# Eleven quadrant products among the last products of the first half, with twelve more weights split ahead and a re-ordered opening, in a single-core streaming encoder layer

## The chip, the core and the metric

One core of a Trainium2 chip runs the whole layer. The metric is the device time of one execution in microseconds (us); of several runs the median is given. A core has five engines that run side by side: TensorE (PE, with the weight load PEld shown apart), VectorE (DVE), ScalarE (ACT), GpSimd (POOL) and SyncE (SP), which here only issues loads.

## The reference, cut to what matters

```python
# x: 2048 prompt rows and 32 sample rows of 1024, all float32
h = rmsnorm(x, ln_g)
q, k, v, gA, B, C, u, gC, mA, mB = split(h @ w_in)      # 1024 x 5376
attn = window_attention(rope(rmsnorm(q)), rope(rmsnorm(k)), v, sink)
conv = causal_conv3(C * u)
yA = (attn * silu(gA)) @ w_attn_out                     # 512 x 1024
yB = (B * conv * silu(gC)) @ w_conv_out                 # 512 x 1024
r  = x + (sigmoid(mA) * yA + sigmoid(mB) * yB) @ w_o    # 1024 x 1024
y  = r + sigmoid(r @ w_ple_gate) * (p @ w_ple_proj)     # 1024 x 1024, 256 x 1024
```

It also returns the last keys and values and the last two rows of `C * u`.

## The kernel before, in words

**Arithmetic.** Each float32 operand is split into a high and a low part that PE multiplies at its fp32r rate, so one product is three matmul passes (high by high, high by low, low by high) accumulated in float32. A split is a copy on ACT (`CAST`, the high part) and a subtraction on DVE (`TENSOR_TENSOR`, the low part); in the projection these are lines 231 and 232, and line 160 is the one line of all instructions in the two stages that are planned by hand. The large products are done in Strassen's manner: a 2 by 2 product of blocks needs seven products, numbered 1 to 7, of sums of blocks. In the second half of the projection the products 2, 3 and 4 are themselves cut into quadrants ("quadrant products", letters A to G).

**Columns.** Rows of x are the moving operand. They are cut into a first half (512 columns of each block) and a second half (528, with the sample rows).

**Stage one, the opening (to about 60 us), planned by hand.** `manual_schedule` holds small generators, one for each piece of work. Each yields which engine comes next and what it needs; `go(gen, due, needs, rank)` puts one on the list, and the planner gives each engine the next instruction by due time and rank (a lower rank goes first), with its own costs (line 115 holds the cost of a POOL instruction, 2.03 for a `pow`). `todo_loads` is the list in which SP issues the loads. `wpp_piece(h)` loads and splits one of four pieces of `w_ple_proj` (tiles wppr, wpp_h); `p_row` loads and splits a row block of p; `x_row(j, k)` loads one of eight row blocks of x for column half j, squares it (sq) and adds it to the running sum of squares; when all eight are in, `stats(j)` starts: the column sum by PE (pr), the `pow` on POOL (rs), and the factors that turn x into h. `wait0` fills PE's time before that with the projection's products of p by `w_ple_proj` (pp), six matmuls each. `sums0` adds up the blocks of the projection's weights for the first group and stores four of the sums to a scratch buffer for the second half.

**Stage two, the projection (to about 890 us).** There are 21 column groups of `w_in`. `steps` is the order of products. For group i of the first half it reads

```python
for i in range(G):
    steps += [[(0, i, 7)], [(0, i, 5)]]
    steps += [[(0, i + 1, 6)]] if i + 1 < G else [[seconds.pop(0)] for _ in range(2)]
    steps += [[(0, i, 3)], [(0, i, 4)]]
```

and after it come the rest of `seconds` (the quadrant products of product 2) and the second half's others. `run_set` (line 767) issues the quadrant products, with tiles la, lb, lc at line 787; the ordinary products stand at lines 649, 651 and 654 with banks a and c and the operands x_h, x_l. A product's weight is a raw tile (wr), loaded by SP, and a split pair (w), of which there are five (`WB = 5`); SP loads eight raw quads ahead ("wf"). In the second half the rows of x are loaded again (xr) and split again while products run. Here the instructions are put in order by a scheduler with a simulated timeline of its own.

**Weights split ahead.** Some weights of stage three are split during stage two and written, high and low together, to a scratch buffer: `halves` has 24 of them (8 of `w_attn_out`, "wa", and 16 of `w_o`, "o"). `half_steps` issues for each, in four places of the order of `steps`: the load by SP, the copy on ACT, the subtraction on DVE, and the store by POOL; `stored` tells stage three that a weight can be read as a finished pair of 512 KB instead of as 256 KB that are split there.

**Stage three (to the end), planned by hand again.** Units of PE work are written out in an order (yB, pp, yA, then the products by `w_o` and `w_ple_gate`, numbered with `UO` and `UPG`, tiles xb_h, xb_l, bank b), and attention tiles are begun at planned times (`begin`), `PRE` = 8 us ahead of a tile's time, with one slot for z at a time (zq, pq). `next_loads` loads a weight as a pair or starts `split_w` when ACT is near enough to idle.

Of the kernel before, what the change touches and what calls it, by code (L numbers as in the profile page):

```python
# [7 lines left out]
F32 = mybir.dt.float32  # L8
# [22 lines left out]
AHEAD = 2  # L31
KP = 41
FIRST = 6
SECOND = 4
EPS = 1e-6
SCALE = 0.125
# [6 lines left out]
def tile_hybrid_stream_step(ctx: ExitStack, tc: tile.TileContext, x, xT, pT, wu, consts, rope, ckT, cv_dup,  # L43
# [60 lines left out]
    def cost(key, op, kw):  # L104
        if LATE["V"]:
            return cost_queue(key, op, kw)
        if op == "dma_start":
            return 0.9 if kw.get("accum_op") is not None else 0.57 if key == "G" else 0.42
        n = size(kw["out"])
        if key == "T":  # L110
            return max(0.109, 0.00044 * n + 0.0064)
        if key == "S":
            return 0.2 + 0.00082 * n + (0.13 if kw.get("accum_out") is not None else 0.0)
        if key == "G":
            return 2.03 if kw.get("op") == ALU.pow else 0.35 + 0.0021 * n
        if op == "tensor_reduce":
            return 0.08 + 0.0012 * size(kw["in_"])
        return 0.3 if n <= 16 else 0.13 + 0.0011 * n
# [162 lines left out]
        open_ = letters(gs, 3, "C") + letters(gs, 4, "C")  # L281
    rest += open_
    for i in range(G):
        steps += [[(0, i, 7)], [(0, i, 5)]]
        steps += [[(0, i + 1, 6)]] if i + 1 < G else [[seconds.pop(0)] for _ in range(2)]
        steps += [[(0, i, 3)], [(0, i, 4)]]
        while begun <= i + AHEAD and begun < G:
            steps += [[(0, begun, p)] for p in ((1,) if begun < FIRST + SECOND else (1, 2))]
            begun += 1
# [67 lines left out]
    def make_sums(g):  # L357
# [9 lines left out]
        for p, i in WS.items():  # L367
# [3 lines left out]
    halves = {("wa", n): dram.tile([P, 2, 4 * P], F32, tag=f"wa{n}", name=f"wa{n}") for n in range(8)}  # L371
    halves.update({("o", n, p): dram.tile([P, 2, 4 * P], F32, tag=f"o{n}_{p}", name=f"o{n}_{p}")
                   for n in range(4) for p in WS})

    def quad_sums(x, n):
        t = {}
# [12 lines left out]
    def half_steps(key, dst):  # L389
        name = "_".join(map(str, key))  # L390
        t = zp.tile([P, 4 * P], F32, tag="z", name=f"z{name}")
        with in_turn(nc.sync.engine):
            if key[0] == "wa":
                nc.sync.dma_start(out=t.rearrange("p (a b) -> p a b", a=4), in_=wu[UY + key[1], :, 0:4, :])
            else:
                nc.sync.dma_start(out=t, in_=quad_sum[UO, key[1]][:, WS[key[2]]])
        yield
        h = zp.tile([P, 4 * P], F32R, tag="z", name=f"h{name}")
        with in_turn(nc.scalar.engine):
            nc.scalar.copy(out=h, in_=t)  # L400
        yield
        with in_turn(nc.vector.engine):
            nc.vector.tensor_tensor(out=t.bitcast(F32R), in0=t, in1=h.bitcast(F32), op=sub)
        yield
        with in_turn(nc.gpsimd.engine):
            nc.gpsimd.dma_start(out=dst[:, 0], in_=h.bitcast(F32))
            nc.gpsimd.dma_start(out=dst[:, 1], in_=t)
        yield

    def stored(key):  # L410
        if key[0] == "q" and key[3] == 0 and key[1] < 2:
            return halves["wa", key[2] - UY]
        if key[0] == "B" and key[2] == UO and key[4] in WS:
            return halves["o", key[3], key[4]]
        return None

    def raw_key(key):
# [496 lines left out]
    def hilo0(h, lo, src, key, after=None):  # L914
        yield {"@": "S"}
        eS.copy(out=h, in_=src)
        yield {"@": "V"}
        eV.tensor_tensor(out=lo, in0=src, in1=h.bitcast(F32), op=sub)
        yield {}
        have0.add(key)  # L920
        if after:
            after()
# [8 lines left out]
    def wpp_piece(h):  # L931
        raw = quad(f"wppr{h}")
        eY.dma_start(out=raw, in_=wu[UPP + h // 2, :, 4 * (h % 2):4 * (h % 2) + 4, :])
        yield {"k": 2}
        wpp[h] = pair(f"wpp{h}")
        go(hilo0(wpp[h][0][:, :512], wpp[h][1][:, :512], raw.rearrange("p a b -> p (a b)"), ("wpp", h), lambda: free("wf")), None, None, -3 if h < 2 else -1)

    def constants():
        eY.dma_start(out=cst, in_=consts)
# [3 lines left out]
    def x_row(j, k):  # L943
        v = B[k // 4, j, k % 4] = xrow(f"b{j}_{k}")
        eY.dma_start(out=v[:, :q0], in_=xT[k * P:(k + 1) * P, j * q0:(j + 1) * q0])
        yield {"k": 1, "@": "S"}
        sq = row(f"sq{j}_{k}")[:, :q0]
        eS.activation(out=sq, in_=v[:, :q0], func=AF.Square, scale=1.0 / 32.0)
        yield {}
        if j not in acc0:  # L950
            acc0[j] = sq
        else:
            yield {"@": "V"}
            eV.tensor_tensor(out=acc0[j], in0=acc0[j], in1=sq, op=add)
            yield {}
            free("k")
        ready[j] = ready.get(j, 0) + 1
        if ready[j] == 8:
            go(stats(j), now[0] + 1.8, None, j * 2 - 3)


    def stats(j):
# [80 lines left out]
    def sums0():  # L1043
        a11, a21, a22, a12 = [quad(f"a0_{i}") for i in range(4)]
        u1, u2 = groups[0][2:]
        for t, (u, s) in zip((a11, a21, a22, a12), ((u1, 0), (u2, 0), (u2, 1), (u1, 1))):
            eY.dma_start(out=t, in_=wu[u, :, 4 * s:4 * s + 4, :])
        yield {"wf": 1}
        sc = quad("sc0")
        for o, x, y in ((sc, a11, a21), (a21, a21, a22), (a11, a11, a21), (a12, a12, a11)):  # L1050
            yield {"@": "V"}
            eV.tensor_tensor(out=o, in0=x, in1=y, op=add)
        yield {}
        sums[0] = {7: sc, 5: a21, 6: a11, 3: a12, 4: a22}
        for p, i in WS.items():
            eG.dma_start(out=wsum[0][:, i], in_=sums[0][p])
        for i in range(NP, NW):
            raw_of[i] = sums[0].pop(worder[i][3])
            go(split0(i), None, None, -0.5)
            yield {}  # L1060
# [9 lines left out]
    def split0(i):  # L1070
        while i > len(made):
# [14 lines left out]
    todo_loads = [({"tmp": 1}, (-2, p_row(0, 0))), ({"tmp": 1}, (-2, p_row(0, 1))), ({"wf": 1}, (-3, wpp_piece(0))),  # L1086
                  ({"wf": 1}, (-2, wpp_piece(1))), ({}, (-2, x_row(0, 0))), ({}, (-2, x_row(0, 1))), ({}, (-2, x_row(0, 2))),
                  ({}, (0, constants())), ({"wf": 1}, (-2, wpp_piece(2)))]
    todo_loads += [({}, (-2, x_row(0, k))) for k in range(3, 8)] + [({"wf": 1}, (-1, wpp_piece(3)))]
    todo_loads += [({"wf": 1}, (0, raw0(i))) for i in range(2)] + [({"tmp": 1}, (0, p_row(1, k))) for k in range(2)]  # L1090
    todo_loads += [({"wf": 1}, (0, raw0(i))) for i in range(2, 5)]
    todo_loads += [({}, (1, x_row(1, k))) for k in range(8)]
    todo_loads += [({"wf": 1}, (-1.5, raw0(i))) for i in range(5, 9)] + [({"wf": 4}, (-0.5, sums0()))]
# [144 lines left out]
    for p, at_ in ((2, (0, G - 1, 2)), (1, (1, pairs_[1], 2, "E")), (6, (1, pairs_[3], 2, "E")), (7, (1, pairs_[5], 2, "E")),  # L1238
# [12 lines left out]
                (spans[0][0] + pitch * j for j in range(len(halves)))]  # L1251
    half_at = sorted((t + lag, j, k) for j, t in enumerate(split_at) for k, lag in enumerate((-11, -2.5, 0.1, 1.0)))
    half_gen = [half_steps(*x) for x in halves.items()]
    conv_at = {(1, G - 2, 1): lambda: conv_load(0), (1, G - 2, 6): lambda: (conv_split(0), conv_load(1)),
               (1, G - 1, 6): lambda: conv_split(1), (1, G - 2, 5): lambda: conv_load(2)}
    conv_at.update({(1, sets[-1], 3 + c % 2, "DE"[c // 2]): lambda c=c: conv_split(2, (c,)) for c in range(4)})
    prep = [at_step[0, g, 7] for g in range(7, G)]
    for i, todo in enumerate(steps):
        if i < NS:
            continue  # L1260
        if todo[0][:2] == (0, 0) and todo[0][2] in (3, 4):
            make_x(todo[0][2])
        run(todo)
        if todo[0] in conv_at:
            conv_at[todo[0]]()
        if i in prep:
            next(X1, None)
        if todo[0] in sums_at:
            quad_sums(*sums_at[todo[0]])
        while half_at and length[i] and half_at[0][0] <= sum(length[:i]):  # L1270
            next(half_gen[half_at.pop(0)[1]])
        if i in after:
            load_second_products(after[i])
        if i in refills:
            if refills[i] == 2:
                for _ in X1:
                    pass
            refill(refills[i])
# [715 lines left out]
    def next_loads():  # L1994
# [36 lines left out]
        while n_split[0] < len(worder) and room["w"] > 0:  # L2031
            i = n_split[0]
            src = stored(worder[i])
            if src is not None:
                if busy["Y"] >= now[0] + 0.5:
                    break
                room["w"] -= 1
                w = wp.tile([P, 2, 4, P], F32R, tag="w", name=f"w{i}")
                W2[i] = w[:, 0], w[:, 1]
                fin[0] = 0.0  # L2040
                eY.dma_start(out=w.bitcast(F32).rearrange("p a b c -> p a (b c)"), in_=src)
                w_ready[i] = fin[0] + 0.5
            else:
                if landed.get(i, 1e9) > now[0] or busy["S"] >= now[0] + (0.3 if i > used[0] + 2 else 1.5):
                    break
                room["w"] -= 1
                go(split_w(i))
            n_split[0] += 1
# [55 lines left out]
    left.update({0: 4, 1: 4, 2: 5, 3: 5})  # L2104
    for e in range(len(TILES)):
        t = (0, 6)[e] if e < 2 else 11 * e if e < 8 else e1 - 40 + 0.96 * (e2 - e1) * (e - 8) / 9
        begin.append((max(0.0, t - PRE), lambda e=e, t=t: go(attention(e, t), None, {"z": 1, "tmp": 2})))
    begin.append((T["yB0_6"], lambda: load_p(2)))
    begin.append((T["yB0_7"], lambda: load_p(3)))
    begin.append((T["yB0_0"], lambda: load_conv(3)))  # L2110
# [103 lines left out]
```

## Time and profile before

| | |
|---|---|
| device time, median of 3 runs | 1509.16 us (1509.11 to 1510.27) |
| profiled execution, its own time | 1508.07 us |
| its span, from first to last instruction | 1506.0 us |
| mean granted TensorE clock | 0.998 of full speed |
| busy: PE, weight load | 1489.3, 1348.6 us |
| busy: DVE, ACT, POOL | 1210.7, 803.7, 399.0 us |
| moved by DMA | 378.34 MB, mean 251 GB/s |

How to read it: a row of the timeline has the start, the length, the engine, the line, the operation, what it writes and reads, its shape and how many in a row, and in brackets the idle time before it with what ended it. A row of the groups has the number of instructions, busy time and mean duration in ns, and the idle time before them with what ended most of it. A row of the windows has a stretch, its length, the busy time of PE, weight load, DVE, ACT and POOL with the number of instructions of each, the granted clock, the DMA share and GB/s. The releaser of a wait is inferred from semaphore events.

### The profile page before, as it was taken

What the parts mean: (1) busy time and instruction counts of PE and PEld (TensorE: products, weight loads), DVE (VectorE), ACT (ScalarE), POOL (GpSimd) and SP (SyncE); (2) the same over time, 40 slices, a digit from 0 to 9 for tenths busy, and PEclk for the clock granted to TensorE, in tenths of its full rate; (3) what the DMA queues carried; (4) which work ended last, traced back from release to release, by engine and by line L of the source; (5) the groups of instructions that cost most, each with busy time, mean ns of one, the idle gap of its engine ahead of it and who ended that gap; (6) DMA issues with size and microseconds to landing.
All of it is one profiled execution on the core that took longest, in us unless ns stands there. A gap on an engine that the chain in (4) does not pass through costs nothing.

```text
span 1506.0 us, 28005 instructions
## 1 busy us (share of the span) xinstructions
PE 1489.3 (99%) x9553; PEld 1348.6 (90%) x9553; DVE 1210.7 (80%) x2308; ACT 803.7 (53%) x1910; POOL 399.0 (26%) x582
## 2 busy tenths in 40 slices
PE   9999999999999999999999999999999999999998
PEld 7878888888889999999999989998888788999998
DVE  7897887885579788799976878778899999676777
ACT  8453244344457655434455646687765686342453
POOL 2133332332211443433323311113232202211201
PEclk9999999999999999999999999999999999999999
DMA  9469886898777987533578885687988959989959
GB/s 353 154 246 348 314 291 221 276 347 271 253 274 256 340 292 262 186 127 122 153 243 312 288 270 181 210 253 218 302 207 272 240 157 258 312 247 283 256 168 286
DMA packets 206670, 378.34 MB, mean 251 GB/s; under 512 B 24896, under 2 KB 58496, under 8 KB 206528
## 3 DMA queue, kind: packets, MB, share of 16 engines
q1 hardware_dynamic: 160608, 258.30, 52.6%
q0 software_dynamic: 36272, 100.44, 22.2%
q10 hardware_dynamic: 9648, 17.83, 3.2%
q8 instruction: 75, 1.23, 0.3%
q14 instruction: 67, 0.55, 0.1%
HBM read 246.53 MB, written 130.04 MB: 250 GB/s over the span
## 4 chain that ended last, share of the span: by engine, by line
PE 91%; DMA 4%; DVE 2%; ACT 1%; issue 1%; POOL 0%; SPq 0%; DVEq 0%; ACTq 0%; POOLq 0%
PE b L160 21%; PE a L654 8%; PE a L651 7%; PE a L649 7%; PE yB L160 6%; PE yA L160 5%; PE la L787 5%; PE c L651 4%; PE c L649 4%; PE c L654 4%; PE lc L787 2%; PE pp L160 2%; PE O L160 2%; PE S L160 2%; PE PT L160 1%; PE lb L787 1%
## 5 line engine op out<-in xcount | busy, mean ns | idle before, releaser
L160 PE MATMUL b<-xb_h,w 128*128 128x264 f32 (+1 forms) x1344 | 310.7, 322 | 1.4 <-DVE at L160 1.4
L160 PEld LDWEIGHTS b<-xb_h,w 128*128 128x128 f32 x1344 | 222.7, 188 | 19.5 <-DVE at L160 1.9
L651 PE MATMUL a<-x_l,w 128*128 128x264 f32 (+1 forms) x744 | 228.2, 320 | 0.0
L649 PE MATMUL a<-x_h,w 128*128 128x264 f32 (+1 forms) x744 | 227.4, 320 | 0.2 <-ACT w L231 0.2
L160 PE MATMUL b<-xb_l,w 128*128 128x264 f32 (+1 forms) x672 | 216.6, 322 | 0.0
L654 PE MATMUL a<-x_h,w 128*128 128x264 f32 (+1 forms) x744 | 199.7, 321 | 0.9 <-DVE w L232 0.9
L231 ACT CAST w<-wr 128x512 fp32r<-128x512 f32 (+1 forms) x180 | 110.5, 619 | 96.2 <-PE c L654 34.9
L232 DVE TENSOR_TENSOR w<-wr,w 128x512 fp32r<-128x512 f32 (+1 forms) x180 | 133.2, 748 | 29.6 <-ACT w L231 28.0
L649 PEld LDWEIGHTS a<-x_h,w 128*128 128x128 f32 x744 | 139.9, 188 | 11.3 <-ACT w L231 0.4
L651 PEld LDWEIGHTS a<-x_l,w 128*128 128x128 f32 x744 | 140.0, 188 | 10.9
L654 PEld LDWEIGHTS a<-x_h,w 128*128 128x128 f32 x744 | 124.0, 188 | 11.9 <-DVE w L232 1.2
L160 PEld LDWEIGHTS b<-xb_l,w 128*128 128x128 f32 x672 | 126.4, 188 | 8.5
L160 ACT CAST w<-wr 128x512 fp32r<-128x512 f32 x120 | 73.6, 622 | 98.4 <-PE b L160 51.5
L787 PE MATMUL la<-x_h,w 128*128 128x264 f32 x516 | 111.3, 285 | 1.6 <-ACT w L231 1.6
L651 PE MATMUL c<-x_l,w 128*128 128x512 f32 (+1 forms) x336 | 110.9, 340 | 0.0
L649 PE MATMUL c<-x_h,w 128*128 128x512 f32 (+1 forms) x336 | 110.5, 339 | 0.0
L231 ACT CAST w<-a 128x512 fp32r<-128x512 f32 x82 | 49.8, 620 | 98.6 <-DVE a L364 33.2
L654 PE MATMUL c<-x_h,w 128*128 128x512 f32 (+1 forms) x336 | 100.1, 339 | 0.0
L160 DVE TENSOR_TENSOR w<-wr,w 128x512 fp32r<-128x512 f32 x120 | 83.6, 705 | 18.0 <-ACT w L160 17.7
L848 DVE SCALAR_TENSOR_TENSOR u<-u,c 128x264 f32<-128x264 f32 (+1 forms) x125 | 59.5, 507 | 42.8 <-ACT u L843 26.1
L160 PE MATMUL yB<-ycs_h,w 128*128 128x264 f32 (+1 forms) x384 | 91.0, 325 | 0.0
L160 PE MATMUL yA<-ac_h,w 128*128 128x264 f32 (+1 forms) x384 | 90.5, 323 | 0.0
(443 smaller groups left out, 3889.7 us busy)
## 6 DMA issues: line engine op xcount, KB each, us to landing
wr<-in_wu SPq DMA_DIRECT2D x161, 256.0 KB, 4.8
a<-in_wu SPq DMA_DIRECT2D x116, 256.0 KB, 5.3
wr<-ws SPq DMA_DIRECT2D x74, 256.0 KB, 4.0
w<-o SPq DMA_DIRECT2D x32, 512.0 KB, 4.7
ws<-a POOLq DMA_DIRECT2D x63, 256.0 KB, 4.3
w<-wa SPq DMA_DIRECT2D x16, 512.0 KB, 5.3
wr<-qs SPq DMA_DIRECT2D x32, 256.0 KB, 4.0
qs<-a POOLq DMA_DIRECT2D x24, 256.0 KB, 5.8
```

The costliest lines, as they stand in the source:

```text
L160: return f(**kw)
L231: nc.scalar.copy(out=hi, in_=src)
L232: nc.vector.tensor_tensor(out=lo, in0=src, in1=hi.bitcast(F32), op=sub)
L649: nc.tensor.matmul(out=ps[:, :cn], lhsT=w[:, 0, k], rhs=x[0][:, c0:c0 + cn], start=first and k == 0, stop=False, skip_group_check=True)
L651: nc.tensor.matmul(out=ps[:, :cn], lhsT=w[:, 0, k], rhs=x[1][:, c0:c0 + cn], start=False, stop=False, skip_group_check=True)
L654: nc.tensor.matmul(out=ps[:, :cn], lhsT=w[:, 1, k], rhs=x[0][:, c0:c0 + cn], start=False, stop=k == 3, skip_group_check=True)
L787: nc.tensor.matmul(out=ps[:, :m], lhsT=w[:, a, k], rhs=r[:, cols], start=q in "ABG" and j == 0 and e == 0, stop=j == 1 and e == 2, skip_gr ...
L848: nc.vector.scalar_tensor_tensor(out=t[:, c0:c0 + cn], in0=t[:, c0:c0 + cn], scalar=-1.0, in1=ps[:, :cn], op0=mul, op1=sub)
```

## The change

- **The order of `steps`.** In the last group of the first half, eleven quadrant products of `seconds` stand behind product 7 (three), 5 (four) and 3 (four); there were two, behind product 5.
- **Weights split ahead.** `halves0` adds twelve (four blocks each of three of the weights of `w_o` and `w_ple_gate`) that stage three uses for its first column half. Their four steps are spread between product 7 of group 14 and product 5 of the last group, with the load four steps ahead, the copy one step ahead, and the subtraction and store at the place.
- **The opening.** All four pieces of `w_ple_proj` have rank -3 (the last two had -1), and the fourth is loaded ahead of the last two row blocks of x; the p rows of block 1 come before the first raw weights. Two of the first eight squares are made on DVE. `stats` is put on the list for 0.3 us after the last sum instead of 1.8. The four stores of `sums0` become a generator of their own with rank 2. The planner's cost of a `pow` goes from 2.03 to 1.1 in this stage.
- **Stage three.** A weight that is needed next may be split when ACT is busy up to 5.0 us ahead (1.5 before), and attention tiles 0 to 2 are begun 11 us ahead of their time instead of 8.

```diff
+H0 = 14
+EARLY = (3, 4, 4, 0)
...
-            return 2.03 if kw.get("op") == ALU.pow else 0.35 + 0.0021 * n
+            return 1.1 if kw.get("op") == ALU.pow else 0.35 + 0.0021 * n
...
     for i in range(G):
-        steps += [[(0, i, 7)], [(0, i, 5)]]
-        steps += [[(0, i + 1, 6)]] if i + 1 < G else [[seconds.pop(0)] for _ in range(2)]
-        steps += [[(0, i, 3)], [(0, i, 4)]]
+        for p, n in zip((7, 5, 3, 4), EARLY if i + 1 == G else (0, 0, 0, 0)):
+            steps += [[(0, i, p)]] + ([[(0, i + 1, 6)]] if p == 5 and i + 1 < G else [[seconds.pop(0)] for _ in range(n)])
...
+    RAW = {1: 0, 4: 1}
+    halves0 = {(x, n, p): dram.tile([P, 2, 4 * P], F32, tag=f"r{x}{n}_{p}", name=f"r{x}{n}_{p}")
+               for x, p in ((UO, 1), (UO, 4), (UPG, 1)) for n in range(4)}
...
+            elif key in halves0:
+                u, e = key[0] + key[1] + 4 * (key[2] == 4), RAW[key[2]]
+                nc.sync.dma_start(out=t.rearrange("p (a b) -> p a b", a=4), in_=wu[u, :, 4 * e:4 * e + 4, :])
...
+        if key[0] == "B" and key[1] == 0:
+            return halves0.get(key[2:])
         return None
...
-        go(hilo0(..., ("wpp", h), lambda: free("wf")), None, None, -3 if h < 2 else -1)
+        go(hilo0(..., ("wpp", h), lambda: free("wf")), None, None, -3)
...
-        yield {"k": 1, "@": "S"}
+        vector = j == 0 and k in (2, 5)
+        yield {"k": 1, "@": "V" if vector else "S"}
         sq = row(f"sq{j}_{k}")[:, :q0]
-        eS.activation(out=sq, in_=v[:, :q0], func=AF.Square, scale=1.0 / 32.0)
+        if vector:
+            eV.scalar_tensor_tensor(out=sq, in0=v[:, :q0], scalar=1.0 / 1024.0, in1=v[:, :q0], op0=mul, op1=mul)
+        else:
+            eS.activation(out=sq, in_=v[:, :q0], func=AF.Square, scale=1.0 / 32.0)
...
-            go(stats(j), now[0] + 1.8, None, j * 2 - 3)
+            go(stats(j), now[0] + 0.3, None, j * 2 - 3)
...
         sums[0] = {7: sc, 5: a21, 6: a11, 3: a12, 4: a22}
-        for p, i in WS.items():
-            eG.dma_start(out=wsum[0][:, i], in_=sums[0][p])
+        kept = dict(sums[0])
+
+        def keep():
+            for p, i in WS.items():
+                eG.dma_start(out=wsum[0][:, i], in_=kept[p])
+                yield {"@": "G"}
+        go(keep(), None, None, 2)
...
-    todo_loads += [({}, (-2, x_row(0, k))) for k in range(3, 8)] + [({"wf": 1}, (-1, wpp_piece(3)))]
-    todo_loads += [({"wf": 1}, (0, raw0(i))) for i in range(2)] + [({"tmp": 1}, (0, p_row(1, k))) for k in range(2)]
+    todo_loads += [({}, (-2, x_row(0, k))) for k in range(3, 6)] + [({"wf": 1}, (-2, wpp_piece(3)))]
+    todo_loads += [({}, (-2, x_row(0, k))) for k in (6, 7)] + [({"tmp": 1}, (-1, p_row(1, k))) for k in range(2)]
+    todo_loads += [({"wf": 1}, (0, raw0(i))) for i in range(2)]
...
+    gen0 = [half_steps(*x) for x in halves0.items()]
+    first0, last0 = at_step[0, H0, 7], at_step[0, G - 1, 5]
+    pitch0 = (last0 - first0) / (len(gen0) - 1)
+    at0 = sorted((first0 + pitch0 * j + lag, j) for j in range(len(gen0)) for lag in (-4, -1, 0, 0.4))
...
+        while at0 and at0[0][0] <= i:
+            next(gen0[at0.pop(0)[1]])
...
-                if landed.get(i, 1e9) > now[0] or busy["S"] >= now[0] + (0.3 if i > used[0] + 2 else 1.5):
+                if landed.get(i, 1e9) > now[0] or busy["S"] >= now[0] + (0.3 if i > used[0] + 2 else 1.5 if i > used[0] + 1 else 5.0):
...
-        begin.append((max(0.0, t - PRE), lambda e=e, t=t: go(attention(e, t), None, {"z": 1, "tmp": 2})))
+        begin.append((max(0.0, t - (PRE if e > 2 else 11.0)), lambda e=e, t=t: go(attention(e, t), None, {"z": 1, "tmp": 2})))
```

More of the change, by code (lines that the diff above doesn't have):

```diff
@@ L935, in wpp_piece @@
         wpp[h] = pair(f"wpp{h}")
-        go(hilo0(wpp[h][0][:, :512], wpp[h][1][:, :512], raw.rearrange("p a b -> p (a b)"), ("wpp", h), lambda: free("wf")), None, None, -3 if h < 2 else -1)
+        go(hilo0(wpp[h][0][:, :512], wpp[h][1][:, :512], raw.rearrange("p a b -> p (a b)"), ("wpp", h), lambda: free("wf")), None, None, -3)
     def constants():
```

## The prediction

> **What bounds the kernel now.** The page first: the busy line, then the chain, then the list of what the matmul engine (PE) waited for.
>
> ```profile
> PE 1489.3 (99%) x9553; PEld 1348.6 (90%) x9553; DVE 1210.7 (80%) x2308; ACT 803.7 (53%) x1910; POOL 399.0 (26%) x582
> PE 91%; DMA 4%; DVE 2%; ACT 1%; issue 1%; POOL 0%; SPq 0%; DVEq 0%; ACTq 0%; POOLq 0%
> PE la L787 <- ACT w L231: 1.6, 2, 1.1
> PE b L160 <- DVE at L160: 1.4, 1, 1.4
> PE pp L160 <- ACT wpp_h L160: 1.4, 1, 1.4
> PE pq L160 <- DMA zq<-z_q: 1.2, 1, 1.2
> PE 1_0_461 L649 <- ACT x_h L160: 1.0, 1, 1.0
> PE lc L787 <- ACT w L231: 1.0, 3, 0.4
> ```
>
> The reader is to see that PE is busy for 1489.3 of 1506.0 us and owns 91% of the chain. The edit takes no matmul away, so all it can win is waiting: the six rows add up to 7.6 us, half a per cent. A change of 0.2% (3.0 us) is about what a measurement of this kernel can tell from none. Each part is therefore held against one of these rows.
>
> **The change part by part.** 1. The opening: the fourth piece of w_ple_proj is loaded two places earlier, all pieces get rank -3, two of the first eight squares go to DVE, and the sum of squares (pr) is planned 1.5 us sooner. The row aimed at is the wait for wpp_h.
>
> ```profile
> 14.40:16.86 2.46, 1.08 (x5) 0.60 (x5) 1.97 (x4) 2.46 (x6) 1.43 (x3) 1.00 1.05 398
> 18.00:21.40 3.40, 3.40 (x10) 2.63 (x9) 2.84 (x6) 1.86 (x4) 2.01 (x3) 0.50 1.05 410
> 4.49 4.04 SPq L160 DMA_DIRECT2D b<-in_xT  x5
> 8.88 0.33 SPq L160 DMA_DIRECT2D wppr<-in_wu  x1
> 8.21 5.40 DMA b<-in_xT
> 10.93 0.63 ACT L160 ACTIVATE sq<-b 128x512 f32<-128x512 f32 x1
> 14.98 0.69 DVE L160 TENSOR_TENSOR sq<-sq,sq 128x512 f32<-128x512 f32 x1
> 15.12 0.62 ACT L160 CAST wpp_h<-wppr 128x512 fp32r<-128x512 f32 x1
> 15.79 0.50 PE L160 MATMUL pp<-p_h,wpp_h 128*128 128x512 f32 x1 [1.38 <-ACT wpp_h L160]
> 16.86 0.95 PE L160 MATMUL pr<-ones,sq 128*128 128x1 f32 x8
> 38.96 1.89 DVE L160 TENSOR_TENSOR w<-wr,w 128x512 fp32r<-128x512 f32 x3
> 40.77 0.68 DVE L160 TENSOR_TENSOR sc<-a,a 128x512 f32<-128x512 f32 x1
> ```
>
> The windows read: length, then busy time of PE, weight load, DVE, ACT, POOL, granted clock, DMA share, GB/s. The eighth row of x was issued at 8.21 and landed at 13.61 (8.21+5.40); the fourth, squared from 10.93, had landed by then, so a load lands every 0.67 us. With wpp moved up two places it lands near 12.9 and is split by about 14.8: PE gets it without a wait. But the last row of x now lands at 14.28, and the squares on DVE stand in DVE's list ahead of sums and of that split. From the sixth row of x on (12.3), DVE has seven operations left: square, two sums, the split, three sums. Back to back, three such operations take 1.89 where one takes 0.68: (1.89-0.68)/2 = 0.61 apart. Seven end at 12.3+6x0.61+0.69 = 16.65, say 16.7. Before, the last sum ended at 14.98+0.69 = 15.67. So pr, at 16.86 now, can run at 16.7: 0.15 us better. PE would do better only if more projection products stood ahead of pr. I followed the planner's own event times by hand, for the order and not for a time: the DVE squares delay its sum by about what the lag gives back, and pr comes behind 39 projection matmuls again. The wait moves from wpp_h to the squares. Bounds: a gain of 1.4 plus the slow clock below; a loss of 0.5, two matmuls of 0.23 fewer ahead of pr. I take -0.15, nearest the DVE rows.
>
> From 18.00 to 21.40 the granted clock is 0.50, and ten 512-column matmuls take what would be half the time: about 1.6 us lost, right after the wait. With a wait of like length I leave it as it is. The Trainium skill (TensorE: Matmul & The Clock Gate, "What's actually happening") says that the clock halves after an idle window of about 3.4 us; the length of the slow stretch agrees with that, but 1.4 us of wait were enough here, so the measurement decides. By the page's rule closing the wait would return the wait alone.
>
> 2. The second column half: pow is planned at 1.1 us, stats(1) 1.5 us sooner, and the four stores of sums stand behind it on POOL (keep), no longer ahead. These stores issue later and nobody waits for them.
>
> ```profile
> 18.24 1.27 POOL L160 TENSOR_TENSOR rs<-rs,nhalf 128x4 f32<-128x4 f32 x1
> 47.47 0.16 DVE L160 TENSOR_SCALAR rs<-pr 128x4 f32<-128x4 f32 x1 [2.88 <-PE pr L160]
> 55.53 0.69 DVE L160 TENSOR_TENSOR s<-2_3_764,s 128x512 f32<-128x512 f32 x1 [3.15 <-issue]
> 55.50:83.00 27.50, 27.50 (x120) 22.17 (x119) 27.25 (x45) 13.96 (x26) 2.70 (x5) 1.00 0.33 116
> 84.62 0.50 PE L649 MATMUL 1_0_461<-x_h,w 128*128 128x512 f32 x1 [1.02 <-ACT x_h L160]
> ```
>
> pow really takes 1.27, so 1.1 is nearer than 2.03. DVE idles 2.88 and 3.15 us around this chain and is then full (27.25 of 27.50) until PE waits at 84.62. Starting the chain 2.4 us sooner (1.5+0.9) fills that idle time; the two squares cost DVE 1.4 us, but before 17 us. The wait of 1.02, with 0.16 of refill, should go: -1.2 (bounds 0 and -1.2).
>
> 3. Eleven quadrant products (there were two) among the last group's products.
>
> ```profile
> 440.00:457.90 17.90, 17.90 (x118) 16.39 (x118) 13.73 (x28) 12.19 (x27) 0.00 (x0) 1.00 0.64 214
> 457.90:473.10 15.20, 15.20 (x125) 15.17 (x124) 14.67 (x34) 10.98 (x27) 3.25 (x6) 1.00 0.75 255
> 473.10:500.00 26.90, 24.36 (x185) 22.91 (x184) 25.82 (x57) 19.98 (x49) 8.06 (x11) 1.00 0.77 258
> 465.93 0.41 ACT L231 CAST w<-wc 128x256 fp32r<-128x256 f32 x1 [1.05 <-PE la L787]
> 491.88 0.64 ACT L231 CAST x_h<-xr 128x528 fp32r<-128x528 f32 x1 [3.39 <-DMA xr<-xc]
> ```
>
> PE loses 2.54 us, from 473.1 on, where DVE is full (25.82 of 26.90) and ACT stands before refilled rows. Where the products are moved (440 to 457.9) PE loses nothing. After the twelfth quadrant product the order is what it was and PE has done the same work. Could DVE have run ahead meanwhile? No: only five weight buffers exist, and at 465.93 ACT still waits for PE to give one back. So the head start can't be stored: 0. Bounds -2.54 and, if the denser splits before 458 cost as much as afterwards (2.54 in 26.9), +1.7 in 17.9.
>
> 4. Twelve more weights split ahead, in groups 14 to 20, read as pairs in the third stage.
>
> ```profile
> 316.00:442.00 126.00, 126.00 (x543) 101.62 (x542) 82.35 (x140) 56.38 (x99) 32.38 (x60) 1.00 0.84 290
> 420.00:440.00 20.00, 20.00 (x87) 16.16 (x87) 16.18 (x33) 11.77 (x22) 4.29 (x8) 1.00 0.98 342
> L160 ACT CAST w<-wr 128x512 fp32r<-128x512 f32 x120 | 73.6, 622 | 98.4 <-PE b L160 51.5
> L160 DVE TENSOR_TENSOR w<-wr,w 128x512 fp32r<-128x512 f32 x120 | 83.6, 705 | 18.0 <-ACT w L160 17.7
> 1180.00:1220.00 40.00, 38.58 (x204) 32.32 (x203) 39.48 (x79) 29.47 (x78) 8.94 (x10) 1.00 0.69 173
> 1203.94 0.50 PE L160 MATMUL b<-xb_h,w 128*128 128x512 f32 x1 [1.43 <-DVE at L160]
> ```
>
> Added in 126 us: 12 x 0.622 = 7.5 us of ACT (56.38 busy), 12 x 0.705 = 8.5 of DVE (82.35 busy), 24 POOL issues, and 12 x 768 KB = 9.4 MB, 75 GB/s on 290. All fits; only 420 to 440 would come to 417, just over the 410 seen at 18 us. Price 0, bounds 0 and +5 (below). In the third stage the same ACT and DVE work goes, against 12 x 256 KB more to load. DVE is full there (39.48 of 40), and PE's one long wait, 1.43 plus 0.16 of refill, is for a late DVE read of a bank. Less DVE work makes it likelier on time, but the planner rewrites the order from there: half of 1.6, -0.8 (bounds 0 and -1.6).
>
> 5. Attention is begun 11 us ahead for the first three tiles: the first two begin at zero either way, and the third needs the single z slot, which the second holds until the first is through. 0; the wait for zq stays. The looser rule for splitting a weight needed next: 0, as no row of the third stage shows PE waiting for a split.
>
> Sum: -0.15-1.2+0+0-0.8 = -2.15. Against the profiled execution, 1508.07, that is 1505.9; it stands 1.09 under the median of the three runs, 1509.16, so 1507.0.
>
> **The rivals.** A. The opening closes. For it: ACT, the engine named, is relieved, and if pr falls seven matmuls later PE covers the sum. Against it: the DVE count. It returns 1.4 and, if the slow clock goes with it, 1.6: 1504.0. By the page's rule on the clock it would be 1505.6.
>
> B. The second half's waits go. For it: DVE works 13.73 of 17.90 us before them, so 4 us lie free. Against it: the five buffers. 2.54 back: 1504.5.
>
> C. Slower: the early splits arrive late. ACT takes its list in order, and an early split's copy waits for its own load as the copy at 491.88 did (3.39). The load is placed three steps ahead of the copy, and in the last group three steps are quadrant products of 0.73 us, not products of 2.8. It decides when ACT stands longer than the five buffers hold out, some 8 us; two such copies, with traffic over 410 GB/s, reach that and cost about 5 us: 1512.2. The Trainium skill (DMA: Bandwidth & Descriptors, "Issuing engines are not separate DMA queues") speaks for C: stores issued by POOL share the engines with SP's loads. No row here separates the two.
>
> D. It gains nothing: each wait removed (84.62, 1203.94) comes back one place later, and the opening loses its 0.5: 1509.6.
>
> **How the numbers follow.** My forecast 0.50, A 0.18, B 0.12, C 0.10, D 0.10. Faster by over 0.2% (under 1506.1): A and B, 0.30, and 0.05 of my own case, whose range is 1505.5 to 1508.5. Slower (over 1512.2): 0.08 of C. The range, 1503.5 to 1510.5, holds my case, D, A and B each alone, and leaves out C and A with B together.
>
> **What would show it.** Step 1: PE's row waiting for wpp_h is gone, one for the squares stands before pr near 15 to 16.7, and the clock is still 0.50 for 3.4 us; if PE is full to 18, A holds. Step 2: no wait at the first L649 product of 1_0, and DVE's 2.88 and 3.15 shorter. Step 3: PE waits from about 470 to 500 as before; under 1 us there means B. Step 4: no PE wait from 316 to 460, ACT waits on the new loads at most 3 us; the wait near 1200 shorter. Step 5: pq still waits for zq near 885. I am wrong most easily where an order is rewritten: the opening's pr, and the third stage.

## The result and the profile after

The changed kernel took 1533.2 us in the median of 4 runs (1528.8 to 1535.5), against 1509.13 us for the kernel before: 1.0157 times as long, 95% interval 1.013 to 1.0183, some 24 us slower. The forecast was 1507.0 us, with 1503.5 to 1510.5 as its range. Two executions of later kernels ran far slower than the rest (4554.15 us with four weights split ahead, 2438.25 us with eight), and the ratios leave them out.

Page of the changed kernel, span and busy line:

```profile
span 1533.7 us, 28071 instructions
PE 1499.8 (98%) x9553; PEld 1354.2 (88%) x9553; DVE 1212.4 (79%) x2310; ACT 801.4 (52%) x1908; POOL 410.1 (27%) x606
```

PE does the same 9553 matmuls, so the time must lie between them. A sum finds the places: for each matmul, the distance from its start to the next one's, less the median distance of its shape. By it the kernel before loses 18.6 us in its execution and the changed one 46.8, and most of the difference sits in few places (its profiled execution, 1535.51 us, was the slowest of the four):

| stretch (us) | lost before | lost after |
|---|---|---|
| 0 to 150 (opening and first products) | 7.8 | 8.0 |
| 400 to 450 (last group of the first half) | -0.1 | 10.4 |
| 450 to 550 (quadrant products) | 5.2 | 4.9 |
| 1100 to 1200 | 0.4 | 2.8 |
| 1200 to 1300 (third stage) | 1.6 | 14.5 |

First place. The timeline of the changed kernel, what PE, ACT and SP did in the last group:

```profile
428.67 0.90 SPq L631 DMA_DIRECT2D xq<-xc  x2
434.94 0.33 SPq L353 DMA_DIRECT2D wr<-in_wu  x1
436.69 0.33 SPq L353 DMA_DIRECT2D wb<-in_wu  x1
437.14 0.84 SPq L649 DMA_DIRECT2D xr<-xc  x2
441.97 0.63 ACT L233 CAST x_h<-xr 128x528 fp32r<-128x528 f32 x1 [6.03 <-DMA xr<-xc]
442.65 0.59 PE L796 MATMUL la<-x_h,w 128*128 128x264 f32 x1 [7.37 <-ACT x_h L233]
447.99 0.63 PE L663 MATMUL a<-x_h,w 128*128 128x512 f32 x1
```

The kernel before, the same loads and its first quadrant product:

```profile
422.32 0.96 SPq L622 DMA_DIRECT2D xq<-xc  x2
424.19 0.33 SPq L352 DMA_DIRECT2D wb<-in_wu  x1
427.39 0.33 SPq L352 DMA_DIRECT2D wr<-in_wu  x1
427.83 0.87 SPq L640 DMA_DIRECT2D xr<-xc  x2
442.13 0.28 PE L787 MATMUL la<-x_h,w 128*128 128x264 f32 x1
```

The first quadrant product (tile la) needs rows of the second half (xr), loaded by SP. Before, they were issued at 427.83, 14 us ahead of their use at 442.13. After, the product is asked for at 435, right behind product 7, and the rows are issued at 437.14: counted from the first load for the row sums (xq, at 419.13 before and 420.43 after), SP's list holds six weight loads ahead of them where it held four. The last two, at 434.94 and 436.69, wait 6.9 us together, by the profile for DVE to give back raw buffers. PE stands 7.37 us and then runs slowly to about 448.4 (a 512-column matmul is shown with 0.63, not 0.40, and the next starts after 0.43, not 0.23; the granted clock was 0.63 from 434.8 to 448.4).

Second place. Third stage of the changed kernel, 30 us before its longest wait (columns as in the prediction), then the timeline:

```profile
1180.00:1210.00 30.00, 29.41 (x147) 24.14 (x146) 18.72 (x36) 14.26 (x39) 9.26 (x10) 1.00 1.08 320
```

```profile
1203.40 0.68 DVE L162 TENSOR_TENSOR c<-c,b 128x512 f32<-128x512 f32 x1
1213.06 0.69 DVE L162 TENSOR_TENSOR c<-c,c 128x512 f32<-128x512 f32 x1 [8.98 <-DMA z_r<-c]
1215.93 0.42 DVE L162 TENSOR_TENSOR ptl<-PT,pth 128x256 fp32r<-128x256 f32 x1
1216.40 0.58 PE L162 MATMUL O<-ptl,VH 128*128 128x256 f32 x1 [6.09 <-DVE ptl L162]
1281.80 0.80 PE L162 MATMUL b<-xb_h,w 128*128 128x512 f32 x1 [2.42 <-DVE c L162]
```

The kernel before, the same 30 us of work:

```profile
1175.00:1205.00 30.00, 28.57 (x147) 23.75 (x146) 29.52 (x56) 19.57 (x53) 8.02 (x8) 1.00 0.90 225
```

DVE is relieved as foreseen (18.72 of 30 us, it was 29.52), but the traffic has gone from 225 to 320 GB/s and the DMA share from 0.90 to 1.08. DVE now stands 8.98 us at a row c until a store from it (z_r<-c), as the profile infers, has landed, and `ptl`, which PE needs, stands behind that in DVE's list. SP issues this store, so it does not issue loads alone. The chain back from PE's wait has the store behind the landing of a new pair (w<-r):

```profile
1192.16 9.00 DMA w<-r
1201.22 11.71 DMA z_r<-c
```

The second wait, 2.42 us at 1281.80 and a stretch at half clock after it, stands by the same chain behind a store to the output that took 8.59 us from 1272.35. The last new pair had landed at 1214.88, so its bytes were not under way then; what makes this store late is open. The DMA view of the 50 us around these stretches, first before, then after, has the median time from issue to landing as its last figure:

```profile
wr<-qs SPq DMA_DIRECT2D x12, 256.0 KB, 3.9
z_r<-c SPq DMA_DIRECT2D x11, 256.0 KB, 4.0
c<-in_xT POOLq DMA_DIRECT2D x9, 256.0 KB, 5.2
```

```profile
w<-r SPq DMA_DIRECT2D x8, 512.0 KB, 8.9
c<-in_xT POOLq DMA_DIRECT2D x12, 256.0 KB, 7.0
z_r<-c SPq DMA_DIRECT2D x9, 256.0 KB, 7.1
wr<-qs SPq DMA_DIRECT2D x9, 256.0 KB, 9.5
```

Eight of the twelve new pairs (w<-r) fall into this stretch, and the transfers shown beside them take longer: a store 7.1 us where it took 4.0.

### The profile page after: what moved, and what is told of

Its sections match the earlier page's. It is cut to its first block, busy times and chain, and to the rows that moved or that the text cites. A ratio compares the mean times of both kernels' runs of the same rounds, so it can differ in the third digit from the quotient of the medians.

```text
span 1533.7 us, 28071 instructions
## 1 busy us (share of the span) xinstructions
PE 1499.8 (98%) x9553; PEld 1354.2 (88%) x9553; DVE 1212.4 (79%) x2310; ACT 801.4 (52%) x1908; POOL 410.1 (27%) x606
## 5 line engine op out<-in xcount | busy, mean ns | idle before, releaser
L234 DVE TENSOR_TENSOR w<-wr,w 128x512 fp32r<-128x512 f32 (+1 forms) x180 | 136.9, 770 | 36.6 <-ACT w L233 36.4
L162 ACT CAST w<-wr 128x512 fp32r<-128x512 f32 x108 | 66.8, 623 | 98.6 <-PE b L162 53.7
L796 PEld LDWEIGHTS la<-x_h,w 128*128 128x128 f32 x516 | 87.1, 189 | 10.5 <-ACT x_h L233 7.8
```

The source lines that it names most:

```text
L162: return f(**kw)
L234: nc.vector.tensor_tensor(out=lo, in0=src, in1=hi.bitcast(F32), op=sub)
L796: nc.tensor.matmul(out=ps[:, :m], lhsT=w[:, a, k], rhs=r[:, cols], start=q in "ABG" and j == 0 and e == 0, stop=j == 1 and e == 2, skip_gr ...
```

## The experiments

The theory to be tested: the wait at 435 comes from the eleven products and the splits together, by the order of SP's list; the waits of the third stage come from reading the pairs where the DMA engines are full. Times below are medians of 4 to 11 runs; ratios are to the kernel before in the same series, where it took 1508.3 to 1509.4 us. The changed kernel's own ratio, 1.0157, is known to some 4 us either way, and so is each difference to it.

**Without the early products.**

```diff
-EARLY = (3, 4, 4, 0)
+EARLY = (0, 2, 0, 0)
```

> The changed kernel with the order of products of before (two quadrant products behind product 5 of the last group); the twelve splits and all else stay. In the changed kernel PE waits 7.4 us at 434.9 for x_h of the first quadrant product: the rows for it (xr) are issued by SP at 437.1, where before issued them at 427.8. Theory T: that wait needs both, products asked for some 15 us sooner and rows loaded 9 us later behind weight loads because the splits hold row tiles; so here the rows come at about 437 as well but the first quadrant product is due only near 450, and the wait (with its slow clock 10.4 us) is gone; the waits of the third stage (8.8 at 1210, 5.7 at 1279) stay. About 1525 us. Rival R1, the products alone are too early: the same here, 1525. Rival R2, the twelve splits by themselves starve the last group: a wait of several us stays near 435 to 450, 1530 or more.

1524.69 us, ratio 1.0102 (1.0089 to 1.0115). The stretch 400 to 450 loses 3.0 us in place of 10.4, none of it in a wait for rows: xr is issued at 429.9. Third-stage waits of 6.1 and 2.0 us are there, as in the changed kernel (6.1 and 2.4). T holds in the time and in the wait that is gone, but not in its reason: the rows do not come at 437, so the early products also push their own rows back in SP's list.

**Without the splits.**

```diff
-               for x, p in ((UO, 1), (UO, 4), (UPG, 1)) for n in range(4)}
+               for x, p in () for n in range(4)}
...
-    pitch0 = (last0 - first0) / (len(gen0) - 1)
+    pitch0 = 0.0
```

> The changed kernel without the twelve new splits (neither made nor read); eleven products stay among the last group's. Theory T: SP issues xr near 428 again, PE waits at most 1 us at 435; third stage without the waits at 1210 and 1279, since the pairs of 512 KB that crowd the DMA queues there are not read. About 1507 to 1509 us. Rival R1 (the products are asked for before their rows can be there, splits or not): a wait of 5 us or more at 435, about 1517. Rival R3 (the waits of the third stage come from the attention tiles begun 11 us ahead or from the looser split rule): they stay, about 1522.

1508.98 us, ratio 0.9996 (0.9987 to 1.0005). SP issues xr at 428.54, PE loses nothing from 400 to 450, and 1.6 us from 1200 to 1300 as before. R1 and R3 fall. The eleven products alone bring nothing that can be measured.

**Without both.** The last two edits together.

> The changed kernel without the splits and with the order of products of before: only the opening, the attention lead and the split rule are left of the change. Theory T: 1506 to 1509 us, no wait at 435, none over 2 us in the third stage. Rival R3: the third stage's 14 us stay, about 1522.

1506.76 us, ratio 0.9990 (0.9981 to 0.9999). With before's order of products or the new one, with the splits or without, four kernels make a square: the early products cost 1.0157 less 1.0102, some 8 us, beside the splits, and 1 us or nothing without them; the splits cost 17 us without the early products and 24 with them.

**Splits made, not read.** The two lines that hand the new pairs to the third stage are left out:

```diff
-        if key[0] == "B" and key[1] == 0:
-            return halves0.get(key[2:])
```

> The changed kernel makes and stores the twelve splits, but the third stage loads and splits these weights itself as before. Theory T: the waits at 1210 and 1279 (14.5 us) are gone, the wait at 435 (10.4 us with its slow clock) stays: about 1519 us. Rival R3: both stay, 1533. Rival R4, making them costs the third stage too (they shift the state in which it begins): in between, over 1523.

1517.4 us, ratio 1.0051 (1.0038 to 1.0064). The waits in the third stage are those of the kernel before (1.33 us at 1213), the one at 435 stays:

```profile
439.92 0.59 PE L794 MATMUL la<-x_h,w 128*128 128x264 f32 x1 [6.12 <-ACT x_h L233]
1215.14 0.50 PE L162 MATMUL b<-xb_h,w 128*128 128x512 f32 x1 [1.33 <-DVE at L162]
```

So reading the pairs costs 1.0157 less 1.0051, 16 us; making them beside the early products costs 8 us. R3 and R4 fall.

**Rows ahead of the last row sums.**

```diff
+            refill(refills[i])
             if refills[i] == 2:
                 for _ in X1:
                     pass
-            refill(refills[i])
```

> The changed kernel, but the rows for the first quadrant products (xr) are loaded before the last two row sums (xq, which serve a later product), no longer behind them. In SP's list xr then stands behind the weight load wr_4260 and ahead of five more weight loads; in the changed kernel it stands behind those five, two of which wait for a weight buffer that PE gives back. Theory T, the wait at 434.9 (7.4 us, 10.4 with the slow clock) is SP's order: xr goes out before 425, the wait is under 1 us, about 1523 to 1524 us, with the third stage's 14.5 us unchanged. Rival R6, the loads are slow because the splits fill the DMA engines in the last group: xr goes out early and still lands after 440, the wait stays over 4 us, 1529 or more.

1525.92 us, ratio 1.0117 (1.0103 to 1.013). SP's list and PE's one wait here:

```profile
418.70 0.93 SPq L649 DMA_DIRECT2D xr<-xc  x2
```

```profile
438.54 0.55 PE L658 MATMUL a<-x_h,w 128*128 128x512 f32 x1 [1.97 <-ACT u L852]
```

The rows go out 18 us sooner, under no less traffic (319 GB/s from 418 to 442, in the changed kernel 292), and the wait for them is gone: SP's order was its cause, R6 falls. (The two loads that hold up the rows in the changed kernel wait for DVE by the profile, not for PE as I had expected.) It was not all: a wait of 1.97 takes its place further on, for a bank that ACT empties (u) behind a weight whose sum DVE made late; the stretch loses 3.9 us, not under 1.

**Splits sooner.**

```diff
-H0 = 14
+H0 = 8
...
-    first0, last0 = at_step[0, H0, 7], at_step[0, G - 1, 5]
+    first0, last0 = at_step[0, H0, 7], at_step[0, 17, 5]
```

> The changed kernel with its twelve splits spread over groups 8 to 17 of the first half, no longer 14 to 20; all of them are read. SP's list in the last group then is that of the kernel without splits. Theory T: the wait at 434.9 falls under 1 us, the waits near 1200 (8.8) and 1270 (5.7) stay: 1523 to 1524 us. Rival R7, it is not where the splits stand but that they exist (more waits in groups 8 to 17): 1527 or more.

1523.5 us, ratio 1.01 (1.0086 to 1.0114). xr is issued at 427.99 and the stretch 400 to 450 loses 0.1 us; one new wait of 1.25 us at 320; the third stage loses 17 us from 1150 to 1300. T holds, R7 falls.

**High halves alone.** The low halves of the new pairs are not read; the high ones are used in their place.

```diff
+                if worder[i][2:] in halves0 and worder[i][1] == 0:
+                    W2[i] = w[:, 0], w[:, 0]
+                    eY.dma_start(out=w[:, 0]..., in_=src[:, 0])
+                else:
...
```

> The changed kernel, but of the twelve new pairs the third stage reads only the high halves (256 KB, as many bytes as a raw weight) and multiplies by them in place of the low ones as well; so ACT and DVE are spared as before and PE does as much, but 3 MB less is read. Theory T: the waits at 1210 and 1279 (14.5 us) come from the DMA engines, full at 320 GB/s from 1180 to 1210; both fall under 2 us each and the time is about 1519 to 1520 us. Rival R5, they come from the order that the planner makes when these splits are missing (DVE's list waits for a row c whatever the traffic): they stay, about 1533.

1520.18 us, ratio 1.0081 (1.0067 to 1.0094): by the ratios 11.5 us less than the changed kernel, with ACT and DVE still spared. Part of that lies elsewhere (in the profiles the opening and the stretch at 435 lose 2.8 us less). From 1100 to 1300 this kernel loses 8.5 us, the changed one 17.3, the one whose pairs are not read 2.7: 9 of 15 us are back. The wait at 1210 shrinks to 1.98 us, the one at 1279 is gone:

```profile
1209.32 0.39 PE L162 MATMUL O<-ptl,VH 128*128 128x256 f32 x1 [1.98 <-DVE ptl L162]
1178.00:1208.00 30.00, 28.92 (x146) 23.86 (x144) 23.61 (x45) 13.77 (x37) 10.10 (x10) 1.00 1.06 294
```

The stretch is still full (1.06, 294 GB/s), for even as 256 KB the pairs come beside raw weights for products eleven places on. The bytes are not the only thing that changed: the planner counts a load's bytes, so SP's list has another order here, and so have the other engines' lists before 1180 and after 1217 (times of the changed kernel). Between these, up to the wait at 1210, DVE and PE have the same instructions in the same order. The store at which DVE stood 8.98 us now takes 7.68 us to land, not 11.71, and is issued 5.4 us before DVE comes to it, not 2.9; DVE stands 2.43 us. So 4.0 of the 6.55 us that DVE is spared are shorter landing, the rest is SP's new order. R5, that the waits stay whatever the traffic, falls; how much of the second wait is bytes and how much order is not shown.

**Four, four others, eight of the twelve.** All with the order of products of before and the splits in groups 8 to 17; the list of weights is `(UO, 1)`, `(UPG, 1)`, or `(UO, 1), (UO, 4)`.

> The order of products of before; only the four weights of w_o's product 1 are split ahead, in groups 8 to 17, and read as pairs near 1100, where before the DMA share was 0.70 at 176 GB/s. The opening and the third stage's rules as in the changed kernel. Theory T: pairs cost nothing where the DMA engines have room, and nothing waits for the splits: no wait over 2 us at 435, 1200 or 1270, about 1506 to 1508 us (the kernel without any of the splits took 1506.8). Rival R8, any pair more costs the third stage: 1510 or more.

1509.97 us, ratio 1.0007 (0.9998 to 1.0016): no gain and no measurable loss against the kernel before. No wait at 435, and none of over 2 us near 1200 or 1270, but one of 2.24 us at 1234. The time lies between T's (to 1508) and R8's (from 1510), and settles neither.

> The order of products of before; only w_ple_gate's product 1 (four weights) split ahead and read as pairs, in the second half of the stretch from 1175 to 1210. Theory T: as with the other four, 1510 to 1515 us. Rival R11: 1519 or more.

1512.79 us, ratio 1.0027 (1.0017 to 1.0038). One wait, of the kind of the changed kernel, 3.98 us at 1198; traffic from 1180 to 1200 is 297 GB/s at a share of 0.99. T's time holds, R11 falls.

> The order of products of before; eight weights (w_o's products 1 and 4) split ahead in groups 8 to 17 and read as pairs; w_ple_gate's product 1 is loaded and split as before. Four pairs in the stretch from 1175 to 1210 where the changed kernel has eight. Theory T: half the added traffic (about 270 GB/s), so less than half of the 14 us: 1510 to 1515 us. Rival R11, the order that the planner makes is the cause, any such weight missing from DVE's list brings the wait: 1519 or more.

1513.58 us, ratio 1.003 (1.0018 to 1.0042); waits of 0.3 to 2.0 us from 1186 to 1262. R11 falls. By the ratios, four pairs near 1100 cost 2.6 us against the kernel without splits, four more near 1180 another 3.5, and the last four on top of these (the kernel without early products, which has twelve but makes them later) about 11. Of these 11, 3.0 are lost at 400 to 450, where the later splits are made; from 1100 to 1300 the losses go from 7.3 to 14.8. The price rises as the stretch fills.

**Raw weights later.**

```diff
-    LEAD, LOOK, SLACK = 2, 11, 1.5
+    LEAD, LOOK, SLACK = 2, 6, 1.5
```

with the splits in groups 8 to 17, and with the early products or the order of before:

> The changed kernel with its twelve splits in groups 8 to 17, all read as pairs, and with raw weights of the third stage loaded 6 weights ahead, no longer 11. In the changed kernel eight pairs are loaded from 1179 to 1204, among them nine raw weights for products up to eleven places later; with 6 most of these come after the pairs, where the traffic had fallen to 126 GB/s (1220 to 1240). Theory T (what hurts is that pairs and later raw weights fall together): 1180 to 1210 goes from 320 to 260 to 290 GB/s, the third stage's waits from 14 to 17 us down to under 6, about 1511 to 1514 us. Rival R9, the pairs alone are too much there, whatever is loaded beside them: 1520 or more. Rival R10, six ahead is too late for raw weights: new waits of PE for weights elsewhere in the third stage.

> The same with the order of products of before. Eleven quadrant products among the others were worth nothing where their rows came in time (0.9996 of before, against 0.9990 with the order of before), so this is within 2 us of the kernel above, whichever theory holds.

1522.47 us, ratio 1.0092 (1.0079 to 1.0105), and 1517.76 us, ratio 1.0055 (1.0043 to 1.0067). This expectation failed. The losses from 1150 to 1300 do fall, from 17 us (splits sooner) to 7, but not by less traffic, so why is open. One of the two times meets R9's 1520, the other does not. In the first, a wait for a raw weight comes in, as R10 had it (ACT stands up to 3.7 us at such a load, DVE behind ACT, PE behind DVE):

```profile
1180.00:1200.00 20.00, 15.88 (x75) 12.79 (x74) 14.11 (x28) 6.94 (x17) 4.91 (x5) 1.00 1.08 338
1330.51 0.81 PE L162 MATMUL b<-xb_h,w 128*128 128x264 f32 x2 [2.80 <-DVE w L162]
```

The two also differ by 4.7 us where I had expected at most 2: in the profiles, 2.6 us among the quadrant products and 3.5 us from 1300 to 1350. In the third stage the two have all but the same order of instructions, so what the early products have to do with the second is open.

No version clearly beats the kernel before. The best, without both, is 0.1% faster, and its interval ends at 0.9999.

## Why the prediction was wrong

**Step 4 failed: its price of 0 for making the splits, and its gain of 0.8 for reading them, were the largest errors.** It weighed the ACT and DVE work of the splits and found both had room, which was right in the main. Two things were left out:

- *Reading.* "12 x 256 KB more to load" was set down and not placed. I showed the window 1180 to 1220, with a share of 0.69, and took the stage by it; the 30 us before its longest wait stood at 0.90, and eight of the twelve loads fall there. The step named DVE as what bounds that stage. DVE was relieved of work, and then stood for stores that land late (11.71 us for the one behind the longest wait). Measured: 16 us for reading the pairs. With half the bytes, 9 of the 15 us lost in the third stage are back, in part through SP's order. The -0.8 that I had booked as a gain is part of that error.
- *Queues moved past.* The splits' loads and their tiles change the order of SP's list in the last two groups. I counted "24 POOL issues" and 75 GB/s, not who stands behind whom on SP. Measured: 8 us, beside the early products.

**Step 3: 0 is right for the products alone** (ratio 0.9996 with, 0.9990 without), and the stretch 450 to 550 loses about 5 us either way, so nothing is stored. The five buffers fit this as the reason, though no run had another number of them. Its upper bound of 1.7 us was wrong, because I priced the moved products by their splits on DVE and never asked when their rows are loaded. Before, xr had 14 us in hand; the move takes 7 of them, and with both parts SP issues the rows 9 us later (437.1), with either part alone 1 to 2 (428.5, 429.9). Each alone fits, both together don't: 8 us.

**Step 1 came out as worked out.** The wait for wpp_h is gone and one for the squares stands before pr, which runs at 16.72 (16.7 forecast); the granted clock is 0.57 from 18 to 22 (0.58 before). That the time fits to 0.02 us is luck: in the twelve other kernels with this opening pr runs between 16.52 and 17.25, so a gain of 0.15 can't be seen.

```profile
16.72 1.02 PE L162 MATMUL pr<-ones,sq 128*128 128x1 f32 x8 [0.92 <-DVE sq L162]
18.00:22.00 4.00, 4.00 (x12) 3.13 (x11) 2.35 (x5) 2.31 (x5) 2.34 (x3) 0.57 1.04 410
```

**Step 2 was a small miss.** The wait of 1.02 for x_h went, but 0.20 for its low part took its place, and 17 us later PE waits 0.75 for a split weight, a wait that the kernel before doesn't have. With the refill after each, 1.3 us were lost before and 1.5 now, so nothing of the 1.2 is gained. That is rival D's mechanism. DVE's 2.88 and 3.15 became 2.74 and 2.32.

```profile
85.62 0.50 PE L660 MATMUL 1_0_471<-x_l,w 128*128 128x512 f32 x1 [0.20 <-DVE x_l L162]
102.43 0.50 PE L658 MATMUL c<-x_h,w 128*128 128x512 f32 x1 [0.75 <-ACT w L233]
```

**Step 5** held in that pq still waits for zq (1.85 us at 899), and the third stage's rules left no trace of their own: in the kernel without both parts its waits are those of before.

**Sums.** Two of the rivals' times are slightly off: C's 5 us on 1507.0 make 1512.0, not 1512.2, and A's 1504.0 still has step 1's 0.15 in it, which A replaces. Neither matters for the account.

**The rivals.** C had the sign, the last group and ACT standing at a late load, and gave it 0.10 and 5 us. The load that came late was not that of a split, as C had it, but that of the rows, behind weight loads in SP's list; and C knew nothing of the third stage, where the larger half was lost. A did not occur (PE waits 0.92 us ahead of pr, and the half clock follows), nor did B: 450 to 550 loses 4.9 us after 5.2 before. The sentence of the Trainium skill that stood for C (DMA: Bandwidth & Descriptors, "Issuing engines are not separate DMA queues") describes the third stage better than the place for which I cited it: transfers issued by SP and by POOL all slowed together there, from 4.0 to 7.1 and from 5.2 to 7.0 us.

## What to carry to other kernels

A step that trades work on an engine for bytes is priced in the stretch where the bytes are read, at that stretch's DMA share, and not by the total or the stage's mean: 3 MB are nothing as a share of 378 MB, but where the engines already stood at 0.90, 9 of 15 lost us came back when they were left out, in part because SP's list changed with them. When work is moved forward, follow each of its inputs back to the issue of its load and ask how much lead that load has; two changes that each eat half of a lead are harmless alone and must be costed together. And where a list is worked off in order, as SP's was here, a new load costs first what it puts ahead of others.

## What the runs showed of the hardware

Waits of PE up to 1.79 us outside the opening left the matmuls after them at full speed in all kernels here. From 1.8 us on most were followed by a stretch at half clock that cost another 1.2 to 2.9 us (1.82 us of wait: 1.5; 7.37 us: 2.9), though 1.85 and 2.24 were not in one case each. The half clock of the opening is something else: of the thirteen kernels with the new opening it is there in eight (1.6 us, after waits of 0.90 to 0.94 us before pr) and missing in five (0.1 or less, after waits of 0.55 to 1.05), so the wait's length alone does not decide it. In the prediction I had tied it to one of 1.4 us.
